# A recurrence in which odd heads change partition halves, so that neighbouring products use different halves of the array's columns

## The chip, the cores and the metric

The kernel runs on one core of one Trainium2 chip. Its engines work side by side: TensorE (PE in the profile; PEld is its loading of weights), VectorE (DVE), ScalarE (ACT), GpSimd (POOL) and SyncE (SP), whose queue issues nearly all DMA loads and stores here. The metric is device time in microseconds (us), as a median over runs.

## The reference

One encoder layer on 1024 tokens of 1024 channels: a half-step SwiGLU block, then two head groups in parallel (four attention heads, and eight heads of an RWKV-7 recurrence with 64 channels each), an output projection, a second SwiGLU block and a norm. What the change touches is the recurrence:

```python
def step(state, inp):
    r_t, w_t, k_t, v_t, aa_t, bb_t = inp
    sa = jnp.einsum('bhvk,bhk->bhv', state, aa_t)
    state = (state * w_t[:, :, None, :] + sa[..., None] * bb_t[:, :, None, :]
             + v_t[..., None] * k_t[:, :, None, :])
    return state, jnp.einsum('bhvk,bhk->bhv', state, r_t)
```

Its state is a 64x64 matrix per head; over the outputs `y` follow a norm per head, a bonus term and a gate. In parallel, attention scores, a softmax and its product with the values are taken in blocks of 128 queries.

## The kernel before

All big weights are streamed from HBM, and most products take several passes over split operands. The stage of the change lies in the middle of the program (lines 1278 to 1482 and the loop over `p` near the end of `tile_layer`).

The 1024 tokens of the recurrence are cut into 16 chunks of 64, worked off in 8 *pairs* `p` of an even (`e` = 0) and an odd (`e` = 1) chunk. Everything about a chunk is precomputed into DRAM, and the class `Pair` loads it: `m1` (decayed receptance and key operands), `TF` (the inverse of the chunk's triangular system), `m3`, and the values `v` twice (into `sv` beside the state, and into `uv` beside the solved rows). `m1` and `TF` have two buffers, by `p % 2`; `m3`, `sv` and `uv` have four for two tiles per pair. So the loads of pair p+2 wait until pair p's last reader, an output product, is done.

`chain` does a step for all 8 heads. Each of its three products contracts 128 partitions and gives 64 rows per head, thus it fills 64 of the array's 128 columns; `rows_of(e)` says which 64 partitions hold the state side `u` and which the value side `v`, and with that which half of the columns a product uses. The three are `ps_z` from `m1` and `sv` (evicted by ACT to `Z`), `ps_z` from `TF` and `Z` (evicted by ACT to `uv`), and `ps_st` from `m3` and `uv` (added by DVE to the next chunk's `sv`, which POOL has filled with the decayed state). Before the change all 8 heads of a step use the same half; the step is cut into two groups of four heads, so that the eviction of one runs beside the products of the other. `outputs` adds two products per head and chunk in `ps_y` (lines 1441 and 1442), in the other half, then norm and gate. `inverse` builds the 64x64 inverses of later pairs from 32x32 blocks with products of 32 columns (`ps_t`).

A scheduler sets the order of instructions on every engine from priorities: `chain` has high priority, and `attend(share)` emits steps of attention (scores `ps_s`, transposes `ps_pt`, values `ps_ov`) so that they fill the time between. The order is fixed when the program is built; each engine and each queue then works in order. When the recurrence and attention are done, `out_in` and `out_proj` (products `ps_wo`) follow.

Of the kernel before, what the change touches and what calls it, by code (L numbers as in the profile page):

```python
# [34 lines left out]
NJ = 4  # L35
# [1242 lines left out]

def rows_of(e):

    return (slice(64, 128), slice(0, 64)) if e == 0 else (slice(0, 64), slice(64, 128))


def half_rows(hh):

    return slice(64 * hh, 64 * hh + 64)
# [40 lines left out]
def inverse(k, pool, p):  # L1329

    nc = k.nc
    x = k.x21[p % 2]
    low = lambda e: slice(64 - 64 * e, 96 - 64 * e)
    high = lambda e: slice(96 - 64 * e, 128 - 64 * e)
    at = lambda e: slice(2 * p + e, 8 * NCH, NCH)
    for e in range(2):
        nc.sync.dma_start(out=x[low(e)], in_=k.xD[at(e), :HL, HL:].rearrange("h s t -> s h t"))
        nc.sync.dma_start(out=k.T11[low(e), :, e], in_=k.tD[at(e)].rearrange("h t c -> t h c"))
        nc.sync.dma_start(out=k.T22[high(e), :, e], in_=k.fD[at(e), HL:, HL:].rearrange("h t c -> t h c"))

    def products(rows, lhs, rhs):
        t = ps(k, "t")[:, : 8 * HL].rearrange("p (h q) -> p h q", q=HL)
        for e in range(2):
            for h in range(8):
                nc.tensor.matmul(t[rows(e), h], lhsT=lhs[:, h], rhs=rhs[:, h, e], start=True, stop=True)  # L1345
        return t

    t = products(high, x, k.T11)
    for e in range(2):
        nc.scalar.copy(out=k.w1[high(e)], in_=t[high(e)])  # L1350
    t = products(low, k.w1, k.T22)
    y = pool.tile([P, 8, HL], F32, name="T12", tag="T12", bufs=1)
    for e in range(2):
        nc.vector.tensor_copy(out=y[low(e)], in_=t[low(e)])
        nc.sync.dma_start(out=k.fD[at(e), :HL, HL:].rearrange("h t c -> t h c"), in_=y[low(e)])


def chain_tools(k, pool):
    k.m1 = [[pool.tile([P, 8, 2, L], F32, name=f"m1{i}{e}") for e in range(2)] for i in range(2)]
    k.TF = [pool.tile([P, 8, P], F32, name=f"TF{i}") for i in range(2)]  # L1360
    k.Z = [pool.tile([P, 8, L], F32, name=f"Z{e}") for e in range(2)]

    k.wl = pool.tile([P, 8, NP2], F32, name="wl")
    for e in range(2):
        for hh in range(2):
            k.nc.gpsimd.tensor_copy(out=k.wl[half_rows(e), hh::2, :], in_=k.WL[half_rows(hh), :, e::2])
        for m in k.m1:
            k.nc.gpsimd.memset(m[e][rows_of(e)[0], :, 0], 0.0)
        k.nc.gpsimd.memset(k.Z[e], 0.0)
    for t in k.TF:  # L1370
        k.nc.gpsimd.memset(t, 0.0)


class Pair:


    def __init__(self, k, pool, p):
        nc = k.nc
        self.k, self.p = k, p
        a, c0 = p // 4, (2 * p) % 8  # L1380
        new = lambda n: [pool.tile([P, 8, L], F32, name=n, tag=n, bufs=4) for _ in range(2)]

        self.m1, self.tf = k.m1[p % 2], k.TF[p % 2]
        for e in range(2):
            u, v = rows_of(e)
            for hh in range(2):
                nc.sync.dma_start(
                    out=self.m1[e][v, hh::2].rearrange("p h s q -> p h (s q)"), in_=k.arD[a][half_rows(hh), :, c0 + e]
                )
            nc.sync.dma_start(out=self.m1[e][u, :, 1], in_=k.akD[a][v, :, p % 4])  # L1390
            nc.sync.dma_start(out=self.tf[u, :, u], in_=k.fD[2 * p + e :: NCH].rearrange("h t c -> t h c"))

        self.m3 = [pool.tile([P, 8, 2, L], F32, name="m3", tag="m3", bufs=4) for _ in range(2)]
        for e in range(2):
            nc.sync.dma_start(out=self.m3[e], in_=k.m3D[a][:, c0 + e])
        self.sv, self.uv = new("sv"), new("uv")
        for e in range(2):
            u, v = rows_of(e)
            for dst in (self.sv[e][u], self.uv[e][v]):
                nc.sync.dma_start(out=dst, in_=k.vD[a][v, p % 4].rearrange("p j (h q) -> p (j h) q", q=L))  # L1400


def chain(k, pool, o, nxt, e):

    nc = k.nc
    hs = [slice(4 * q, 4 * q + 4) for q in range(2)]
    u, v = rows_of(e)
    m1, m3, sv, uv, Z = o.m1[e], o.m3[e], o.sv[e], o.uv[e], k.Z[e]
    after = o.sv[1] if e == 0 else (nxt.sv[0] if nxt else None)

    def products(name, lhs, rhs, then):
        t = h8(ps(k, name))
        for q in hs:
            for h in range(q.start, q.stop):
                nc.tensor.matmul(t[u, h], lhsT=lhs[:, h], rhs=rhs[:, h], start=True, stop=True)  # L1415
            then(q, t[u, q])

    products("z", m1[:, :, 1], sv, lambda q, t: nc.scalar.copy(out=Z[u, q], in_=t))
    if after is not None:
        w = k.wl[v, :, o.p : o.p + 1].broadcast_to([64, 8, L])  # L1420
        nc.gpsimd.tensor_tensor(out=after[u], in0=sv[v], in1=w, op=ALU.mult)
    products("z", o.tf[:, :, u], Z, lambda q, t: nc.scalar.copy(out=uv[u, q], in_=t))
    if after is not None:
        products(
            "st", m3[:, :, 1], uv,
            lambda q, t: nc.vector.tensor_tensor(out=after[u, q], in0=t, in1=after[u, q], op=ALU.add),
        )


def outputs(k, pool, o):  # L1430

    nc = k.nc
    p = o.p
    yp = []

    def output(e):
        if not yp:
            yp.append(h8(ps(k, "y")))
        v = rows_of(e)[1]
        for h in range(8):  # L1440
            nc.tensor.matmul(yp[0][v, h], lhsT=o.m1[e][:, h, 0], rhs=o.sv[e][:, h], start=True, stop=False)  # L1441
            nc.tensor.matmul(yp[0][v, h], lhsT=o.m3[e][:, h, 0], rhs=o.uv[e][:, h], start=False, stop=True)  # L1442

    st = pool.tile([P, 2, 8], F32, name="gst", tag="gst", bufs=3)
    bc = lambda x: x[:, :, None].broadcast_to([P, 8, L])
    yc = pool.tile([P, HB], F32, name="yc", tag="yc", bufs=3)
    a, c = p // 4, slice((p % 4) * P, (p % 4 + 1) * P)

    def last():
        output(1)  # L1450
        nc.vector.tensor_reduce(out=st[:, 0], in_=yp[0], axis=AX.X, op=ALU.add)
        nc.vector.tensor_scalar(out=st[:, 0], in0=st[:, 0], scalar1=1.0 / L, scalar2=None, op0=ALU.mult)
        nc.vector.tensor_tensor(out=h8(yc), in0=yp[0], in1=bc(st[:, 0]), op=ALU.subtract)

    x = []

    def norm():
        x.extend(pool.tile([P, NJ, P], F32, name=n, tag=n, bufs=2) for n in ("lgx", "box"))
        nc.sync.dma_start(out=x[0], in_=k.lgD[a][:, :, c])
        nc.sync.dma_start(out=x[1], in_=k.boD[a][:, :, c])  # L1460
        sq = pool.tile([P, HB], F32, name="ysq", tag="ysq", bufs=1)
        nc.scalar.activation(out=sq, in_=yc, func=AF.Square)
        nc.vector.tensor_reduce(out=st[:, 1], in_=h8(sq), axis=AX.X, op=ALU.add)
        nc.vector.tensor_scalar(
            out=st[:, 1], in0=st[:, 1], scalar1=1.0 / L, scalar2=GN_EPS, op0=ALU.mult, op1=ALU.add
        )
        newton(k, pool, st[:, 1])
        nc.gpsimd.tensor_tensor(out=h8(yc), in0=h8(yc), in1=bc(st[:, 1]), op=ALU.mult)

    def gate():  # L1470
        lg, bo = x
        t = ps(k, "yt")
        for j in range(NJ):
            nc.tensor.transpose(t[:, j * P : (j + 1) * P], yc[:, j * P : (j + 1) * P], k.ident)
        nc.vector.tensor_tensor(out=lg, in0=t.rearrange("p (j q) -> p j q", q=P), in1=lg, op=ALU.mult)
        nc.gpsimd.tensor_tensor(out=lg, in0=lg, in1=bo, op=ALU.add)
        nc.gpsimd.dma_start(out=k.ybD[a][:, :, c], in_=lg)

    return lambda: output(0), last, norm, gate

# [97 lines left out]
def tile_layer(ctx, tc, I, out):  # L1580
# [176 lines left out]
    with pool_("inv", "left") as ip, pool_("chain") as pool:  # L1757
# [3 lines left out]
        inverse(k, ip, 1)  # L1761
        chain_tools(k, pool)
        ops = [Pair(k, pool, 0)]
        nc.gpsimd.memset(ops[0].sv[0][rows_of(0)[1]], 0.0)
        late = None
        for p in range(NP2):
            o = ops.pop(0)
            even, odd, norm, gate = outputs(k, pool, o)
            with tc.high_priority(offset=1500):
                chain(k, pool, o, None, 0)  # L1770
            if p + 2 < NP2:
# [5 lines left out]
            attend((p + 0.45) / 9.2)  # L1777
            with tc.high_priority(offset=1500):
                chain(k, pool, o, ops[0] if ops else None, 1)
            with tc.high_priority(offset=0):  # L1780
                even()
            attend((p + 1.21) / 9.2)

            def late(odd=odd, norm=norm, gate=gate):
                with tc.high_priority(offset=0):
                    odd()
                    norm()
                    gate()

# [127 lines left out]
```

## Time and profile before

| | us |
|---|---|
| median of 3 runs | 2118.7 (2116.01 to 2120.11) |
| profiled execution | 2118.3 |
| its span | 2116.5 |
| PE busy | 2038.9 (96%) |
| DVE busy | 1551.8 (73%) |
| ACT busy | 924.4 (44%) |
| POOL busy | 252.8 (12%) |
| TensorE clock granted, mean | 0.982 |

A row of the profile names the line, the engine, the operation and its tiles as out<-in. A busy PE is not PE at its peak, since products are pipelined: a row with x8 in 0.63 us holds eight products that overlap, and their pace is the distance of the starts. A fp32 product appears as two entries. The whole program's span is told in the page; the stage of the recurrence lies between about 1115 and 1342 us.

### The profile page before, as it was taken

What the parts mean: (1) busy time and instruction counts of PE and PEld (TensorE: products, weight loads), DVE (VectorE), ACT (ScalarE), POOL (GpSimd) and SP (SyncE); (2) the same over time, 40 slices, a digit from 0 to 9 for tenths busy, and PEclk for the clock granted to TensorE, in tenths of its full rate; (3) what the DMA queues carried; (4) which work ended last, traced back from release to release, by engine and by line L of the source; (5) the groups of instructions that cost most, each with busy time, mean ns of one, the idle gap of its engine ahead of it and who ended that gap; (6) DMA issues with size and microseconds to landing.
All of it is one profiled execution on the core that took longest, in us unless ns stands there. A gap on an engine that the chain in (4) does not pass through costs nothing.

```text
span 2116.5 us, 28417 instructions
## 1 busy us (share of the span) xinstructions
PE 2038.9 (96%) x10496; PEld 1650.0 (78%) x10496; DVE 1551.8 (73%) x2718; ACT 924.4 (44%) x1614; POOL 252.8 (12%) x259
## 2 busy tenths in 40 slices
PE   7999999999999999998988999999999999999998
PEld 4788878887888767766767888787888888878887
DVE  6999996579896677889774666576655556599975
ACT  5543343344443466652244444555433333453333
POOL 1100000000001254432133222111000000000001
PEclk8999999999999999999999999999999999999999
DMA  8277732235332124445436764651222222253322
GB/s 330 92 238 242 246 118 94 94 117 183 115 114 95 65 65 122 134 130 139 99 87 157 192 168 137 210 186 37 100 80 82 78 80 90 100 194 110 105 70 80
DMA packets 189771, 273.74 MB, mean 129 GB/s; under 512 B 77504, under 2 KB 121920, under 8 KB 189632
## 3 DMA queue, kind: packets, MB, share of 16 engines
q1 hardware_dynamic: 187920, 268.62, 40.6%
q0 software_dynamic: 1280, 3.15, 0.5%
q8 instruction: 83, 1.36, 0.3%
q14 instruction: 56, 0.46, 0.1%
q10 hardware_dynamic: 432, 0.15, 0.0%
HBM read 202.66 MB, written 66.58 MB: 127 GB/s over the span
## 4 chain that ended last, share of the span: by engine, by line
PE 80%; DVE 11%; DMA 3%; issue 2%; ACT 2%; POOL 1%; SPq 1%; DVEq 0%; ACTq 0%; POOLq 0%
PE ps_w L66 39%; PE ps_dn L66 21%; PE ps_in L66 5%; PE ps_wo L66 4%; DVE Tpr L1317 2%; PE ps_ov L1230 2%; PE ps_z L1415 2%; PE ps_s L66 1%; DVE T L1321 1%; PE ps_pt L1222 1%; PE ps_y L1442 1%; PE ps_y L1441 1%; DVE pair L60 1%; DMA h<-x 1%; PE ps_t L1345 1%
## 5 line engine op out<-in xcount | busy, mean ns | idle before, releaser
L66 PE MATMUL ps_w<-pair 128*128 128x512 f32 x3744 | 877.4, 396 | 13.1 <-ACT pair L59 9.7
L66 PEld LDWEIGHTS ps_w<-pair 128*128 128x128 f32 x3744 | 706.0, 189 | 181.7 <-ACT pair L59 10.3
L66 PE MATMUL ps_in<-pair,win 128*128 128x512 f32 x960 | 253.9, 415 | 8.2 <-DVE acc L1069 4.1
L60 DVE TENSOR_TENSOR pair<-raw,pair 128x512 fp32r<-128x512 f32 x256 | 177.1, 700 | 108.3 <-ACT pair L59 108.2
L59 ACT CAST pair<-raw 128x512 fp32r<-128x512 f32 x256 | 155.4, 621 | 222.3 <-PE ps_w L66 176.8
L66 PE MATMUL ps_dn<-pair 128*128 128x512 f32 x1008 | 236.6, 393 | 2.7 <-DVE part L608 1.7
L66 PEld LDWEIGHTS ps_in<-pair,win 128*128 128x128 f32 x960 | 184.0, 195 | 59.2 <-issue 10.9
L66 PEld LDWEIGHTS ps_dn<-pair 128*128 128x128 f32 x1008 | 188.9, 188 | 47.5 <-DVE part L608 2.5
L66 PE MATMUL ps_dn<-pair,dh 128*128 128x512 f32 (+1 forms) x704 | 204.2, 375 | 0.0
L66 PEld LDWEIGHTS ps_dn<-pair,dh 128*128 128x128 f32 x704 | 128.1, 188 | 25.8 <-issue 0.7
L388 ACT COPY part<-ps_w 128x512 f32<-128x512 f32 x120 | 70.1, 585 | 168.1 <-PE ps_w L66 159.3
L66 PE MATMUL ps_dn<-pair,dl 128*128 128x512 f32 (+1 forms) x352 | 131.2, 375 | 0.0
L551 DVE SCALAR_TENSOR_TENSOR h<-ps_dn,mod,h 128x512 f32<-128x512 f32 (+1 forms) x128 | 90.4, 713 | 37.8 <-PE ps_dn L66 37.5
L59 ACT CAST pair<-hraw 128x512 fp32r<-128x512 f32 x124 | 73.2, 620 | 69.9 <-DMA hraw<-hidD 30.7
L206 POOL TENSOR_TENSOR nacc<-nacc,nsq 128x512 f32<-128x512 f32 x12 | 17.7, 1472 | 666.8 <-ACT nsq L202 666.8
L138 DVE SCALAR_TENSOR_TENSOR wmod<-wmod,cact 128x1024 f32<-128x1024 f32 x68 | 82.8, 1220 | 9.5 <-DMA wmod<-w_mod 9.1
L486 DVE TENSOR_TENSOR t<-ps_w,part 128x512 f32<-128x512 f32 x80 | 54.5, 687 | 46.7 <-PE ps_w L66 28.0
L60 DVE TENSOR_TENSOR pair<-hraw,pair 128x512 fp32r<-128x512 f32 x124 | 82.9, 685 | 5.2 <-ACT pair L59 4.8
L699 POOL TENSOR_TENSOR h<-h,nr 128x256 f32<-128x256 f32 (+1 forms) x6 | 5.4, 915 | 649.0 <-ACT nr L229 649.0
L66 PE MATMUL ps_wo<-pair,woh 128*128 128x512 f32 x256 | 79.8, 393 | 0.0
L66 PEld LDWEIGHTS ps_dn<-pair,dl 128*128 128x128 f32 x352 | 66.3, 188 | 12.8 <-issue 0.2
L481 DVE TENSOR_TENSOR c<-ps_w,part 128x512 f32<-128x512 f32 x80 | 53.3, 685 | 29.5 <-PE ps_w L66 24.4
(348 smaller groups left out, 3089.5 us busy)
## 6 DMA issues: line engine op xcount, KB each, us to landing
wmod<-w_mod SPq DMA_DIRECT2D x68, 512.0 KB, 4.4
raw<-ffn_w_gate SPq DMA_DIRECT2D x44, 512.0 KB, 3.6
raw<-ffn_w_up SPq DMA_DIRECT2D x44, 512.0 KB, 4.5
hidD<-c SPq DMA_DIRECT2D x44, 512.0 KB, 2.7
hraw<-hidD SPq DMA_DIRECT2D x44, 512.0 KB, 3.4
draw<-ffn_w_down SPq DMA_DIRECT2D x40, 512.0 KB, 3.7
h<-x SPq DMA_DIRECT2D x32, 256.0 KB, 4.6
hD<-h SPq DMA_DIRECT2D x32, 256.0 KB, 2.0
```

The lines of the kernel that those rows point to most:

```text
L59: k.nc.scalar.copy(out=hi, in_=src)
L60: k.nc.vector.tensor_tensor(out=lo, in0=src, in1=hi.bitcast(F32), op=ALU.subtract)
L66: k.nc.tensor.matmul(out, lhsT=x, rhs=y, start=start, stop=stop, skip_group_check=onto)
L138: k.nc.vector.scalar_tensor_tensor(out=w, in0=w, scalar=1.0, in1=k.cact, op0=ALU.mult, op1=ALU.mult, accum_out=m)
L388: nc.scalar.copy(out=t, in_=x)
L481: nc.vector.tensor_tensor(out=c[i][:, j], in0=x, in1=y, op=ALU.add)
L486: nc.vector.tensor_tensor(out=t, in0=x, in1=y, op=ALU.add)
L551: nc.vector.scalar_tensor_tensor(out=y, in0=x, scalar=gt[:, d : d + 1], in1=y, op0=ALU.mult, op1=ALU.add)
L1222: nc.tensor.transpose(tp[:, q : q + P], pr[:, s0 + q : s0 + q + P], k.ident)
L1230: nc.tensor.matmul(x.po[:, cols], lhsT=pt[:, b * P : (b + 1) * P], rhs=k.v[b][:, cols], start=b == 0, stop=b == x.i)
L1317: nc.vector.tensor_tensor(out=v, in0=T[:, 0:t, 0:t].rearrange("p s c -> p c s"), in1=xp[:, 0:t, t][:, None, :].broadcast_to([P, t, t]), op ...
L1415: nc.tensor.matmul(t[u, h], lhsT=lhs[:, h], rhs=rhs[:, h], start=True, stop=True)
```

## The change

For odd heads (`hh` = 1) the sides `u` and `v` are exchanged, so that heads h and h+1 of a step give their results to different column halves. A step's product is no longer cut into two groups of heads but issues all eight, alternating; `Z` is one tile of 128 partitions by 4 head pairs, evicted at once; `TF` holds two heads per tile (an even and an odd one, block-diagonal). One of the two evictions to `uv` goes to DVE. The loads of `akD`, `fD`, `m3D` and `vD` are cut by head parity. Output products of both chunks are issued together, alternating by chunk, after the odd chunk. `inverse` loops over heads outside and chunks inside.

```diff
+def rows_of(e, hh=0):
+    return (slice(64, 128), slice(0, 64)) if e == hh else (slice(0, 64), slice(64, 128))
...
     def products(rows, lhs, rhs):
         t = ps(k, "t")[:, : 8 * HL].rearrange("p (h q) -> p h q", q=HL)
-        for e in range(2):
-            for h in range(8):
+        for h in range(8):
+            for e in range(2):
...
             for hh in range(2):
+                u, v = rows_of(e, hh)
...
-            nc.sync.dma_start(out=self.m1[e][u, :, 1], in_=k.akD[a][v, :, p % 4])
-            nc.sync.dma_start(out=self.tf[u, :, u], in_=k.fD[2 * p + e :: NCH].rearrange("h t c -> t h c"))
+                nc.sync.dma_start(out=self.m1[e][u, hh::2, 1], in_=k.akD[a][own, hh::2, p % 4])
+                nc.sync.dma_start(
+                    out=self.tf[e][u, :, u], in_=k.fD[2 * p + e + NCH * hh :: 2 * NCH].rearrange("h t c -> t h c")
+                )
...
-            nc.sync.dma_start(out=self.m3[e], in_=k.m3D[a][:, c0 + e])
+            src = k.m3D[a][:, c0 + e]
+            nc.sync.dma_start(out=self.m3[e][:, 0::2], in_=src[:, 0::2])
+            for dst, own in zip(rows_of(e, 1), rows_of(e)):
+                nc.sync.dma_start(out=self.m3[e][dst, 1::2], in_=src[own, 1::2])
...
-            for dst in (self.sv[e][u], self.uv[e][v]):
-                nc.sync.dma_start(out=dst, in_=k.vD[a][v, p % 4].rearrange("p j (h q) -> p (j h) q", q=L))
+            src = k.vD[a][rows_of(e)[1], p % 4].rearrange("p j (s q) -> p j s q", q=L)
+            for hh in range(2):
+                u, v = rows_of(e, hh)
+                for dst in (self.sv[e][u], self.uv[e][v]):
+                    nc.sync.dma_start(out=dst[:, hh::2], in_=src[:, :, hh])
...
+    sides = [(hh, slice(hh, 8, 2), *rows_of(e, hh)) for hh in range(2)]
+
+    def products(name, lhs, rhs):
+
+        t = ps(k, name)[:, : NJ * L].rearrange("p (j q) -> p j q", q=L)
+        for h in range(8):
+            u = sides[h % 2][2]
+            nc.tensor.matmul(t[u, h // 2], lhsT=lhs(h, u), rhs=rhs(h), start=True, stop=True)
+        return t
+
+    t = products("z", lambda h, u: m1[:, h, 1], lambda h: sv[:, h])
+    z = pool.tile([P, NJ, L], F32, name="Z", tag="Z", bufs=2)
+    nc.scalar.copy(out=z, in_=t)
     if after is not None:
...
+        for hh, hs, u, v in sides:
+            w = k.wl[v, hs, o.p : o.p + 1].broadcast_to([64, NJ, L])
+            nc.gpsimd.tensor_tensor(out=after[u, hs], in0=sv[v, hs], in1=w, op=ALU.mult)
+    t = products("z", lambda h, u: tf[:, h // 2, u], lambda h: z[:, h // 2])
+    for hh, hs, u, v in sides:
+        (nc.vector.tensor_copy if hh else nc.scalar.copy)(out=uv[u, hs], in_=t[u])
     if after is not None:
...
+        t = products("st", lambda h, u: m3[:, h, 1], lambda h: uv[:, h])
+        for hh, hs, u, v in sides:
+            nc.vector.tensor_tensor(out=after[u, hs], in0=t[u], in1=after[u, hs], op=ALU.add)
...
+    def output():
+        yp.append(h8(ps(k, "y")))
         for h in range(8):
...
+            for i, (lhs, rhs) in enumerate(((o.m1, o.sv), (o.m3, o.uv))):
+                for e in range(2):
+                    nc.tensor.matmul(
+                        yp[0][rows_of(e)[1], h], lhsT=lhs[e][:, h, 0], rhs=rhs[e][:, h], start=i == 0, stop=i == 1
+                    )
```

How the order moves, on PE first, at the odd chunk of the first pair. Before: products of a step in fours, output products of one chunk between.

```order
L1442 MATMUL ps_y_9661<-uv_9517,m3_9511 64x64
L1415 MATMUL ps_z_9627<-sv_9516,m101_9483 64x64 x4
L1415 MATMUL ps_z_9639<-Z1_9489,TF0_9486 64x64 x4
L1222 MATMUL ps_pt_8948<-ident_60,pr_8915 128x128 x2
L1441 MATMUL ps_y_9661<-sv_9516,m101_9483 64x64
L1415 MATMUL ps_z_9639<-Z1_9489,TF0_9486 64x64 x4
L1415 MATMUL ps_st_9650<-uv_9518,m3_9512 64x64 x4
L1442 MATMUL ps_y_9661<-uv_9518,m3_9512 64x64
```

The same place now; `sv_9527` and `uv_9529` are of the even chunk, `sv_9528` and `uv_9530` of the odd one.

```order
L1230 MATMUL ps_ov_9040<-v2_8268,pt_9034 128x128
L1424 MATMUL ps_st_9681<-uv_9530,m3_9520 64x64
L1455 MATMUL ps_y_9776<-uv_9530,m3_9520 64x64
L1455 MATMUL ps_y_9776<-sv_9527,m100_9482 64x64
L1455 MATMUL ps_y_9776<-sv_9528,m101_9483 64x64
L1455 MATMUL ps_y_9776<-uv_9529,m3_9519 64x64
L1424 MATMUL ps_st_9681<-uv_9530,m3_9520 64x64 x7
```

The steps come in eights, and the output products of both chunks stand together at the end of the odd chunk.

On SP, the last part of the loads of the second pair (`m3`, `sv`, `uv`; `oD` is a store of attention, `fD<-T12` a result of `inverse`). Before:

```order
L1391 DMA TF1_9487<-fD_129 64x8x64
L1395 DMA m3_9615<-m3D0_114 128x1024
L1395 DMA m3_9616<-m3D0_114 128x1024
L1254 DMA oD0_122<-ot_8944 512x1x128
L1355 DMA fD_129<-T12_9602 32x8x32 x2
L1400 DMA sv_9619<-vD0_118 64x512
L1400 DMA uv_9621<-vD0_118 64x512
L1400 DMA sv_9620<-vD0_118 64x512
L1400 DMA uv_9622<-vD0_118 64x512
```

Now:

```order
L1400 DMA m3_9637<-m3D0_114 128x4x128
L1402 DMA m3_9637<-m3D0_114 64x4x128 x2
L1400 DMA m3_9638<-m3D0_114 128x4x128
L1356 DMA fD_129<-T12_9620 32x8x32 x2
L1402 DMA m3_9638<-m3D0_114 64x4x128 x2
L1254 DMA oD0_122<-ot_9062 512x1x128
L1409 DMA sv_9645<-vD0_118 64x4x64
L1409 DMA uv_9647<-vD0_118 64x4x64
```

The last two rows come twice for each chunk: 26 loads of a pair where there were 14.

At the end of the stage, also on SP: `h` and `wo` are loads of the output projection, `oD` the store of an attention block (`ot`), the seventh of eight blocks before:

```order
L1508 DMA h4_0_11585<-hD0_84 128x512 x2
L1254 DMA oD1_123<-ot_11639 512x1x128
L1508 DMA h6_0_11586<-hD0_84 128x512
L1510 DMA wo_11781<-w_out 128x1024
L1508 DMA h6_0_11586<-hD0_84 128x512
L1510 DMA wo_11817<-w_out 128x1024
```

and the eighth, the last, now:

```order
L1523 DMA h4_0_11701<-hD0_84 128x512 x2
L1254 DMA oD1_123<-ot_11870 512x1x128
L1525 DMA wo_11897<-w_out 128x1024
L1523 DMA h6_0_11702<-hD0_84 128x512 x2
L1525 DMA wo_11933<-w_out 128x1024
```

The first load of `wo` stands behind the store of the last attention block. On PE there are now no score products (`ps_s`) after the last `ps_y`, and 35 rows of them (seven sets of five) before the change.

## Rows read from the trace of the kernel before

**Rows 1.** Windows: stretch, length, then busy us and instructions of each engine, clock, DMA share.

```profile
1132.90:1309.10 176.20, 174.54 (x2147) 152.79 (x2147) 104.76 (x392) 77.99 (x198) 41.47 (x39) 0.99 0.62 160
1309.10:1341.70 32.60, 28.74 (x196) 24.99 (x196) 24.63 (x78) 18.56 (x37) 3.76 (x4) 1.00 0.60 202
1179.98:1189.23 9.25, 9.25 (x115) 7.87 (x116) 6.76 (x28) 4.41 (x11) 2.36 (x4) 1.00 1.00 255
1120.00:1140.00 20.00, 14.80 (x175) 12.99 (x173) 10.06 (x45) 9.38 (x26) 4.61 (x5) 0.82 0.70 171
```

**Rows 2.** Order of time on PE: start us, us, engine, line, what, count.

```profile
1140.76 0.27 PE L1442 MATMUL ps_y<-uv,m 128*64 128x64 f32 x1
1140.81 0.22 PE L1415 MATMUL ps_st<-uv,m 128*64 128x64 f32 x1
1140.87 0.22 PE L1442 MATMUL ps_y<-uv,m 128*64 128x64 f32 x1
1140.87 0.22 PE L1415 MATMUL ps_st<-uv,m 128*64 128x64 f32 x1
...
1146.70 0.63 PE L1415 MATMUL ps_z<-sv,m 128*64 128x64 f32 x8
1147.16 0.63 PE L1415 MATMUL ps_z<-Z,TF 128*64 128x64 f32 x8
1147.72 0.44 PE L1222 MATMUL ps_pt<-ident,pr 128*128 128x128 f32 x2
...
1138.19 1.10 PE L1345 MATMUL ps_t<-T,x 128*32 128x32 f32 x32
```

**Rows 3.** Groups by shape on PE: count, busy us, mean ns, idle before.

```profile
L1442 PE MATMUL ps_y<-uv,m 128*64 128x64 f32 x256 | 33.3, 227 | 0.0
...
L1415 PE MATMUL ps_st<-uv,m 128*64 128x64 f32 x240 | 19.6, 225 | 0.1
...
L1345 PE MATMUL ps_t<-T,w 128*32 128x32 f32 x256 | 10.7, 203 | 0.9 <-ACT w L1350 0.9
```

**Rows 4.** Tile sv: DVE's adds, duration ns min/median/max.

```profile
L1426 DVE TENSOR_TENSOR sv<-ps_st,sv x30: 406/427/429, 1141.3 to 1301.7; 64x256 f32<-64x256 f32 x30
```

**Rows 5.** Lines 1395 and 1400 on SP: issue ns min/median/max; landing of line 1400.

```profile
L1395 SPq DMA_DIRECT2D m<-m3D x16: 375/558/721, 1125.9 to 1268.3; - x16
...
L1400 SPq DMA_DIRECT2D uv<-vD x16: 450/587/913, 1127.6 to 1270.6; - x16
...
DMA to landing us min/median/max: 2.7/5.1/7.0
```

**Rows 6.** SP in order of time, and its waits from 1179 to 1189 us.

```profile
1185.17 0.45 SPq L1337 DMA_DIRECT2D x<-xD  x1
1187.95 0.30 SPq L1339 DMA_DIRECT2D T<-fD  x1
...
SPq L1339 <- DMA m<-m3D: 1.9, 1, 1.9
```

**Rows 7.** PE in order of time, the recurrence's first product.

```profile
1132.89 0.77 PE L1415 MATMUL ps_z<-sv,m 128*64 128x64 f32 x5 [2.80 <-DMA sv<-vD]
```

**Rows 8.** The stage's end: order of time, and lines 1244, 1510, tile woh.

```profile
1328.94 0.44 PE L1222 MATMUL ps_pt<-ident,pr 128*128 128x128 f32 x2 [0.68 <-ACT ot L1252]
...
1340.72 1.06 PE L1230 MATMUL ps_ov<-v,pt 128*128 128x128 f32 x8
...
1327.66 0.60 PE L1250 MATMUL ps_ot<-ident,o 128*128 128x128 f32 x4
...
1328.30 0.58 ACT L1252 COPY ot<-ps_ot 128x512 f32<-128x512 f32 x1 [0.50 <-PE ps_ot L1250]
...
L1244 ACT ACTIVATE o<-o,oss x8: 713/722/724, 1143.0 to 1347.6; 128x512 f32<-128x512 f32 x8
...
DMA to landing us min/median/max: 3.4/4.3/5.8
...
L59 ACT CAST woh<-wo x16: 1034/1050/1054, 1338.7 to 1422.0; 128x1024 fp32r<-128x1024 f32 x16
```

More of the change, by code (lines that the diff above doesn't have):

```diff
@@ L1273, in attention @@
     return [lambda i=i, h=h: step(i, h) for i in blocks for h in range(NH)] + [lambda: step(blocks[-1], NH), lambda: transposed(state[3])]
-def rows_of(e):
-    return (slice(64, 128), slice(0, 64)) if e == 0 else (slice(0, 64), slice(64, 128))
+def rows_of(e, hh=0):
+    return (slice(64, 128), slice(0, 64)) if e == hh else (slice(0, 64), slice(64, 128))
 def half_rows(hh):
@@ L1359, in chain_tools @@
     k.m1 = [[pool.tile([P, 8, 2, L], F32, name=f"m1{i}{e}") for e in range(2)] for i in range(2)]
-    k.TF = [pool.tile([P, 8, P], F32, name=f"TF{i}") for i in range(2)]
-    k.Z = [pool.tile([P, 8, L], F32, name=f"Z{e}") for e in range(2)]
+    k.TF = [[pool.tile([P, NJ, P], F32, name=f"TF{i}{e}") for e in range(2)] for i in range(2)]
     k.wl = pool.tile([P, 8, NP2], F32, name="wl")
@@ L1365, in chain_tools @@
         for hh in range(2):
[L1366 to L1371, printed above, removed]
+            u, v = rows_of(e, hh)
+            k.nc.gpsimd.tensor_copy(out=k.wl[v, hh::2, :], in_=k.WL[half_rows(hh), :, e::2])
+            for m in k.m1:
+                k.nc.gpsimd.memset(m[e][u, hh::2, 0], 0.0)
+    for two in k.TF:
+        for t in two:
+            k.nc.gpsimd.memset(t, 0.0)
 class Pair:
@@ L1384, in __init__ @@
         for e in range(2):
-            u, v = rows_of(e)
+            own = rows_of(e)[1]
             for hh in range(2):
+                u, v = rows_of(e, hh)
                 nc.sync.dma_start(
@@ L1394, in __init__ @@
         for e in range(2):
-            nc.sync.dma_start(out=self.m3[e], in_=k.m3D[a][:, c0 + e])
+            src = k.m3D[a][:, c0 + e]
+            nc.sync.dma_start(out=self.m3[e][:, 0::2], in_=src[:, 0::2])
+            for dst, own in zip(rows_of(e, 1), rows_of(e)):
+                nc.sync.dma_start(out=self.m3[e][dst, 1::2], in_=src[own, 1::2])
         self.sv, self.uv = new("sv"), new("uv")
         for e in range(2):
-            u, v = rows_of(e)
-            for dst in (self.sv[e][u], self.uv[e][v]):
-                nc.sync.dma_start(out=dst, in_=k.vD[a][v, p % 4].rearrange("p j (h q) -> p (j h) q", q=L))
+            src = k.vD[a][rows_of(e)[1], p % 4].rearrange("p j (s q) -> p j s q", q=L)
@@ L1403, in chain @@
+            for hh in range(2):
+                u, v = rows_of(e, hh)
+                for dst in (self.sv[e][u], self.uv[e][v]):
+                    nc.sync.dma_start(out=dst[:, hh::2], in_=src[:, :, hh])
 def chain(k, pool, o, nxt, e):
     nc = k.nc
-    hs = [slice(4 * q, 4 * q + 4) for q in range(2)]
-    u, v = rows_of(e)
-    m1, m3, sv, uv, Z = o.m1[e], o.m3[e], o.sv[e], o.uv[e], k.Z[e]
+    m1, m3, sv, uv, tf = o.m1[e], o.m3[e], o.sv[e], o.uv[e], o.tf[e]
     after = o.sv[1] if e == 0 else (nxt.sv[0] if nxt else None)
[L1411 to L1416, printed above, removed]
@@ L1418, in chain @@
-    products("z", m1[:, :, 1], sv, lambda q, t: nc.scalar.copy(out=Z[u, q], in_=t))
-    if after is not None:
-        w = k.wl[v, :, o.p : o.p + 1].broadcast_to([64, 8, L])
-        nc.gpsimd.tensor_tensor(out=after[u], in0=sv[v], in1=w, op=ALU.mult)
-    products("z", o.tf[:, :, u], Z, lambda q, t: nc.scalar.copy(out=uv[u, q], in_=t))
+    sides = [(hh, slice(hh, 8, 2), *rows_of(e, hh)) for hh in range(2)]
[5 more added lines that the diff above has]
+        return t
@@ L1423, in chain @@
     if after is not None:
[L1424 to L1427, printed above, removed]
+        t = products("st", lambda h, u: m3[:, h, 1], lambda h: uv[:, h])
+        for hh, hs, u, v in sides:
+            nc.vector.tensor_tensor(out=after[u, hs], in0=t[u], in1=after[u, hs], op=ALU.add)
 def outputs(k, pool, o):
@@ L1434, in outputs @@
     yp = []
[L1436 to L1439, printed above, removed]
+    def output():
+        yp.append(h8(ps(k, "y")))
         for h in range(8):
-            nc.tensor.matmul(yp[0][v, h], lhsT=o.m1[e][:, h, 0], rhs=o.sv[e][:, h], start=True, stop=False)
-            nc.tensor.matmul(yp[0][v, h], lhsT=o.m3[e][:, h, 0], rhs=o.uv[e][:, h], start=False, stop=True)
+            for i, (lhs, rhs) in enumerate(((o.m1, o.sv), (o.m3, o.uv))):
[3 more added lines that the diff above has]
+                    )
     st = pool.tile([P, 2, 8], F32, name="gst", tag="gst", bufs=3)
@@ L1449, in last @@
     def last():
-        output(1)
+        output()
         nc.vector.tensor_reduce(out=st[:, 0], in_=yp[0], axis=AX.X, op=ALU.add)
@@ L1477, in gate @@
         nc.gpsimd.dma_start(out=k.ybD[a][:, :, c], in_=lg)
-    return lambda: output(0), last, norm, gate
+    return last, norm, gate
 def out_in(k, pool, y, a):
@@ L1763, in tile_layer @@
         ops = [Pair(k, pool, 0)]
-        nc.gpsimd.memset(ops[0].sv[0][rows_of(0)[1]], 0.0)
+        for hh in range(2):
+            nc.gpsimd.memset(ops[0].sv[0][rows_of(0, hh)[1], hh::2], 0.0)
         late = None
@@ L1767, in tile_layer @@
             o = ops.pop(0)
-            even, odd, norm, gate = outputs(k, pool, o)
+            last, norm, gate = outputs(k, pool, o)
             with tc.high_priority(offset=1500):
@@ L1779, in tile_layer, with late @@
                 chain(k, pool, o, ops[0] if ops else None, 1)
-            with tc.high_priority(offset=0):
-                even()
             attend((p + 1.21) / 9.2)
-            def late(odd=odd, norm=norm, gate=gate):
+            def late(last=last, norm=norm, gate=gate):
                 with tc.high_priority(offset=0):
-                    odd()
+                    last()
                     norm()
```

## The prediction

> **What bounds the kernel now.** The page says that TensorE is busy nearly everywhere, so I went straight to the stage of the change with the windows view, then to the groups by shape, the order of time on PE, the SP queue, and last the end of the stage. From the first product of the recurrence (1132.9 us) to the last output product (1309.1) PE is busy 174.5 of 176.2 us at a clock of 0.99, while DVE has 104.8, ACT 78.0, POOL 41.5 and the DMA engines a share of 0.62 [rows 1]. So PE bounds this stretch, by instruction slots: a fp32 product is two passes, and I call a pass what the trace counts. Eight passes into one half of the columns start 0.46 us before the next eight (1146.70, 1147.16): 57.5 ns each. But where state products (L1415 ps_st, one half) meet output products (L1442, other half), starts come at 1140.76, .81, .87, .87: two passes per 57 ns, 29 ns each [rows 2], though both use all 128 rows. That is what the change wants everywhere.
>
> **Passes.** ps_z and ps_y have two groups each of 256 passes, of which one stands in rows 3, and ps_st has 240 [rows 3]: 1264. At some 30 seams like the one above about three passes are already free, 90 in all (an estimate from that seam and the order). Now (1264 - 90) x 57.5 ns = 67.5 us; alternating, 1264 x 28.75 = 36.3 us. Saved: 31 us. The 512 passes of 32 columns (two groups of 256) run at (1.10 - 0.20)/31 = 29 ns within one column block [rows 2], so alternating may bring between nothing and half, 0 to 8 us. I take 3, below the middle, since 29 ns is also the closest pace that the 64-column rows show. The Trainium skill (TensorE: Matmul & The Clock Gate, "Wait — 56ns, not 53.3ns?") says that starts never come closer than about 25 ns however few columns there are; by it these save at most 512 x 4 ns = 2 us. The trace shows no run of closer starts.
>
> **Switches of shape.** Leaving a 64-column run costs 0.16 us instead of 0.0575 (last pass of 1147.16 at 1147.56, next shape at 1147.72), and entering one costs about the same. In the order of PE the runs of 64-column products that 128-column work follows fall from 63 to 47: 16 x 0.2 to 0.3, I take 4 us. In all PE sheds 38 us.
>
> **Other engines.** Z is evicted once over 128 partitions instead of twice over 64, so ACT does less. One of two uv copies goes to DVE, an operation like the add of 0.43 us [rows 4]: 16 of them, 7 us on an engine with 71 us idle. POOL's decay product is split with the same elements. I cost these at nothing, hidden under PE; where a DVE queue of small operations stands before an add, a step waits up to 1 us, which is inside the 4 us below.
>
> **Loads, what the change adds.** A pair had 14 loads, now 26, of the same bytes: akD, fD and the v rows in halves, m3 in three. An issue of the SP queue takes 0.56 us for 512 KB and 0.59 for 128 KB [rows 5], so size hardly matters: 12 x 0.55 = 6.6 us more per pair (bounds: 12 x 0.30, the shortest issue in rows 6, is 3.6; 12 x 0.6 is 7.2). A pair's SP work is now some 14 x 0.55 plus about ten others at 0.5 = 13 us in a period of 176.2/8 = 22 us; it becomes 19 to 20. The pieces are 256 and 512 bytes long instead of 2 and 4 KB; no row separates sizes, so between nothing and double for 1.5 MB at the 255 GB/s of a saturated load (DMA share 1.00, rows 1), 6 us a pair; I take 2. PE needs (156 - 11)/7 = 20.7 us per pair (next paragraph), so the loads stay just under it; I give 4 us in all for their jitter, bounds 0 and 25. The first pair has no cover: its first product, at 1132.89, had waited 2.8 us for sv [rows 7]. In the new order 16 issues instead of 8 lie between the zeroing of TF and that sv: 8 x 0.55 = 4.4, less one wait that runs beside it: first product at 1136.5.
>
> **The end of the stage.** Before, 32.6 us lie between the last output product and pure ps_wo work [rows 1], and attention fills them. The order of the change has put all score products of this tail ahead of the recurrence's end; what stays is three steps of transposes and values. Before, these ran from 1328.94 to 1341.78, 12.8 us [rows 8]; the other 19.8 us move ahead, some 2 of them before the first product. So the recurrence is 176.2 - 38 + 18 = 156 us of PE, and ends at 1136.5 + 156 + 4 (loads) + 4 (the last two steps have nothing beside them: six hand-overs at 0.6 to 0.7) = 1300.5.
> Then something comes that was hidden. SP's first wo load now stands behind the oD store of the last attention block; before, behind that of the block ahead. That last block must be scaled (last values at 1341.78, o ready at 1348.3: 6.5 us), transposed (0.64), copied (0.58) and stored (an issue of 0.6), then wo lands in 4.3 us and is split in 1.05 [rows 8]: 13.7 us in which PE has four transposes. After such a gap PE runs for a while at the lower of its two levels, 1.2 GHz instead of 2.4: the 20 us of the start, with a gap like it, have a mean of 0.82 [rows 1], which is 3.6 us lost; with one gap of less work I take 2. ps_wo alone starts at 1300.5 + 12.8 + 13.7 + 2 = 1329.0 instead of 1341.7. Everything behind it moves with it: 12.7 us.
>
> **Sum.** The profiled execution took 2118.3 us (span 2116.5), 0.4 below the median of 2118.7. 2118.7 - 12.7 = 2106.
>
> **Rivals.**
> - *The cover holds better.* The values overlap the wait for wo or the o chain ends earlier, and loads cost nothing: 38 less 3.6 for the start, 4 for the steps and 2 to 5 at the end: 2091. For it: DVE and ACT have room. Against it: PE's and SP's orders are fixed, and the store stands before wo.
> - *The loads become the bound (slower).* After 1185.62 SP issued nothing until 1187.95, when an m3 load had landed [rows 6]: the queue holds only some eight loads in flight, and v loads land in 5.1 us, up to 7.0 [rows 5]. With 36 loads a pair, eight in flight: 36 x 5.1/8 = 23 us a pair; at 4.2 us it is 19. The pair after next can't be loaded before this pair's output products, so the wait isn't caught up. Gain and loss meet at a pair of 20.7 + (12.7 + 4)/7 = 23.1 us; at 24.5 the time is 2118.7 + 7 x 1.4 = 2128. For it: a DMA share of 1.00 in a load burst. Against it: halves land sooner than wholes, and most bursts had slack.
> - *The alternation does little.* The mechanism: loading of weights for the other half waits for the running pass, and 29 ns holds only over a seam of a few passes. Then 34 of the 38 us are missing: 2140. Against it: the pairs of starts in rows 2; no row shows more than six in a sequence. The Trainium skill (the same page, "The mechanism") says that loading overlaps a running product only when the row groups differ, and here they don't; it speaks for this rival, and the trace of the seam against it.
>
> **Chances.** Forecast 0.50, better cover 0.22, loads 0.21, little 0.07. The forecast's own range is 2097 to 2116; with the others 2089 to 2125 holds eight in ten. About 0.2% (4 us) can be told from no change. Faster by more: nearly all of the first two and a fifth of the loads' case, 0.74. Within: 0.02 of the forecast and 0.07 of the loads, 0.09. Slower: the rest of the loads' case and the last, 0.17.
>
> **What would show it.** ps_z, ps_st and ps_y starting in pairs, 29 ns per pass, over whole groups of 16; fewer than 95% busy PE between first and last recurrence product; SP busy for most of that stretch; no score products after the last ps_y, and a gap of some 12 us on PE before the first ps_wo with a lower clock behind it. It is wrong if that gap is short (then faster), if PE waits on "DMA sv<-vD" at several pairs (then slower), or if passes of a group stay 57 ns apart.

## The result: slower by 0.7%

| | before | after |
|---|---|---|
| median of 4 runs | 2119.4 us (2116.01 to 2120.53) | 2134.1 us (2131.0 to 2137.12) |
| ratio | | 1.0071, 95% interval 1.0055 to 1.0088 |
| span of the profiled execution | 2116.5 | 2129.1 |
| PE busy, clock granted | 2038.9, 0.982 | 2017.1, 0.976 |

TensorE works less and the program takes longer. The windows of the changed kernel, first product to last output product and from there to the first ps_wo, answer to [rows 1]; the third line holds both stretches, and the fence behind it has the same for the kernel before.

```profile
1135.00:1327.30 192.30, 166.84 (x2240) 140.53 (x2241) 120.15 (x441) 72.26 (x178) 42.80 (x53) 0.93 0.58 147
1327.30:1352.00 24.70, 10.81 (x88) 9.36 (x84) 15.39 (x47) 11.48 (x21) 4.04 (x5) 0.82 0.69 222
1135.00:1352.00 217.00, 177.65 (x2321) 149.89 (x2321) 135.54 (x488) 83.73 (x199) 46.84 (x57) 0.92 0.60 155
```

```profile
1132.90:1340.20 207.30, 201.78 (x2331) 176.36 (x2331) 128.21 (x470) 96.04 (x235) 45.24 (x43) 0.99 0.62 168
```

PE's busy time fell by 24.1 us (201.8 to 177.7), but its idle time grew from 5.5 to 39.4, so the stretch is 9.7 us longer, and it began 2.1 us later. The profiled execution of the change is the fastest of its four (2131.0 us), so its trace shows a little less than the difference of the medians.

The alternation itself works. PE in order of time (start, us) against [rows 2]: 14 passes of ps_z in 0.65 us, where 8 took 0.63. The last row, 27 us on, is the first product of the next pair.

```profile
1187.78 0.24 PE L1424 MATMUL ps_z<-sv,m 128*64 128x64 f32 x1 [1.62 <-DMA sv<-vD]
1187.79 0.27 PE L1455 MATMUL ps_y<-sv,m 128*64 128x64 f32 x1
1187.86 0.22 PE L1424 MATMUL ps_z<-sv,m 128*64 128x64 f32 x1
1187.89 0.22 PE L1455 MATMUL ps_y<-sv,m 128*64 128x64 f32 x1
1188.19 0.65 PE L1424 MATMUL ps_z<-sv,m 128*64 128x64 f32 x14
1188.77 0.81 PE L66 MATMUL ps_s<-kn,qh 128*128 128x512 f32 x2
1189.38 0.63 PE L66 MATMUL ps_s<-kn,ql 128*128 128x512 f32 x1
1189.81 0.63 PE L1197 MATMUL ps_s<-kr,qr 128*128 128x512 f32 x1
...
1214.93 0.33 PE L1424 MATMUL ps_z<-sv,m 128*64 128x64 f32 x2 [0.75 <-DMA sv<-vD]
```

The same groups by shape (count, busy us, mean ns, idle before) as in [rows 3]: a ps_y group has 21.5 us busy instead of 33.3, ps_st 14.6 instead of 19.6.

```profile
L1455 PE MATMUL ps_y<-uv,m 128*64 128x64 f32 x256 | 21.5, 227 | 0.0
L1424 PE MATMUL ps_z<-sv,m 128*64 128x64 f32 x256 | 16.0, 241 | 10.5 <-DMA sv<-vD 7.3 <-DVE nwt L245 1.6 <-DVE sv L1440 0.9
L1424 PE MATMUL ps_st<-uv,m 128*64 128x64 f32 x240 | 14.6, 235 | 4.5 <-DVE uv L1436 2.6 <-ACT uv L1436 1.9
```

What sets the pace is seen where the pairs begin: at 1187.78 and 1214.93, 27 us apart, the first product waits for sv, which only just landed. With the pairs counted from 0, the distance over pairs 1 to 7 is 25.0 us (1163.1 to 1313.2); before the change it was 22.4 (1155.1 to 1289.3). PE's waits for sv in the stretch (us in total, times, longest):

```profile
PE ps_z L1424 <- DMA sv<-vD: 7.3, 5, 3.1
```

SP in order of time, answering to [rows 5, 6], shows why sv is late.

```profile
1168.84 0.53 SPq L1389 DMA_DIRECT2D m<-arD  x1
1169.41 0.61 SPq L1392 DMA_DIRECT2D m<-akD  x1
1170.07 0.61 SPq L1393 DMA_DIRECT2D TF<-fD  x1
...
1194.60 0.58 SPq L1389 DMA_DIRECT2D m<-arD  x1
...
1201.19 0.61 SPq L1392 DMA_DIRECT2D m<-akD  x1
1204.82 0.57 SPq L1254 DMA_DIRECT2D oD<-ot  x1
...
1211.42 0.57 SPq L1409 DMA_DIRECT2D sv<-vD  x1
1212.04 1.63 SPq L1409 DMA_DIRECT2D uv<-vD  x1
1213.71 0.62 SPq L1409 DMA_DIRECT2D sv<-vD  x1
1214.37 0.61 SPq L1409 DMA_DIRECT2D uv<-vD  x1
...
L1409 SPq DMA_DIRECT2D sv<-vD x32: 573/607/1398, 1131.8 to 1312.4; - x32
...
L1402 SPq DMA_DIRECT2D m<-m3D x32: 573/607/1427, 1127.5 to 1307.7; - x32
```

SP hardly rests: an issue of a load starts some 0.65 us after the one before, 0.61 of issue and mostly 0.04 to the next. Between the first load of pair 2 (1168.84) and that of pair 3 (1194.60) it issues 37 transfers, 23.4 us of issue in 25.8 us, without a pause of more than 0.2 us. In the next pair, a store that waits for its data holds the queue on top (oD, 3.0 us at 1201.8). Before, there were on average 24 issues a pair, 13.8 us in 21.3. Two other reasons for a late load, a buffer that isn't free and a queue that is full, are not seen in this trace. Between the first and the last product, SP never waits longer than 1.0 us for a product of PE, which is how a buffer comes free (up to 3.6 before). And counted at the end of each issue from 1130 to 1310 us, at most seven of SP's transfers are on their way, four in the median; before the change eight was the most, and at 1185.62, where the prediction saw SP stand still, it was eight.

The end of the stage answers to [rows 8]: PE waits for the scaled o, then for wo.

```profile
1338.17 1.06 PE L1230 MATMUL ps_ov<-v,pt 128*128 128x128 f32 x8
1344.33 1.12 PE L1250 MATMUL ps_ot<-ident,o 128*128 128x128 f32 x4 [5.10 <-ACT o L1244]
1352.01 0.79 PE L66 MATMUL ps_wo<-pair,woh 128*128 128x512 f32 x1 [6.57 <-ACT woh L59]
```

### The profile page after: what moved, and what is told of

The parts are those of the page before. It is cut to its first block, busy times and chain, and to the rows that moved or that the text cites. A ratio compares the mean times of both kernels' runs of the same rounds, so it can differ in the third digit from the quotient of the medians.

```text
span 2129.1 us, 28518 instructions
## 1 busy us (share of the span) xinstructions
PE 2017.1 (95%) x10496; PEld 1624.4 (76%) x10496; DVE 1560.7 (73%) x2734; ACT 913.1 (43%) x1582; POOL 255.9 (12%) x279
## 4 chain that ended last, share of the span: by engine, by line
PE 72%; DVE 15%; DMA 6%; issue 3%; ACT 2%; SPq 2%; POOL 0%; DVEq 0%; ACTq 0%; POOLq 0%
PE ps_w L66 32%; PE ps_dn L66 20%; PE ps_in L66 5%; PE ps_wo L66 4%; DVE Tpr L1318 2%; DVE wmod L138 2%; DVE pair L60 2%; DMA wmod<-w_mod 2%; PE ps_s L66 1%; PE ps_ov L1230 1%; DVE T L1322 1%; PE ps_x L951 1%; PE ps_z L1424 1%; PE ps_pt L1222 1%; DMA sv<-vD 1%
## 5 line engine op out<-in xcount | busy, mean ns | idle before, releaser
L59 ACT CAST pair<-hraw 128x512 fp32r<-128x512 f32 x124 | 73.4, 620 | 69.8 <-DMA hraw<-hidD 30.3
```

The source lines that it names most:

```text
L59: k.nc.scalar.copy(out=hi, in_=src)
```

## Experiments

Three theories were put up. A: the number of issues on SP is the bound. B: the transfers are, the same bytes in small pieces. C: turn-around, the longer chain of hand-overs and the buffers. Each time is a median; the ratio is to runs of the kernel before on the same chip.

**The loads alone, in the kernel before.**

```diff
...
-            nc.sync.dma_start(out=self.m3[e], in_=k.m3D[a][:, c0 + e])
+            src = k.m3D[a][:, c0 + e]
+            nc.sync.dma_start(out=self.m3[e][:, 0::2], in_=src[:, 0::2])
+            for r in rows_of(e):
+                nc.sync.dma_start(out=self.m3[e][r, 1::2], in_=src[r, 1::2])
...
```

> The kernel before with only the loads of the change: akD, fD and v in halves by head parity, m3 in three pieces, 26 loads per pair instead of 14, into the same places as before (no exchange of halves, products as before). Theory A and B alike (the loads alone are what costs): SP needs 25 to 26 us per pair against PE's 22.3, so the stage ends 7 x 3 = 21 us later: 2140 (2133 to 2146), with PE waiting for sv at most pairs. Theory C (the longer chain, the merged output products or the exchange costs, not the loads): 2119 +- 3.

2136.3 us, 1.0083 (1.0070 to 1.0096): the loads alone cost as much as the whole change, with the products, the chain and the buffers of the kernel before. So C falls. Pairs come 26.5 us apart (1157.6 to 1316.8). The first products wait for sv here too, but not for long, since more of attention's products stand between them (2258 products from the first to the last of the recurrence, 2147 before). PE's waits (us, times, longest):

```profile
PE ps_z L1423 <- DMA sv<-vD: 4.6, 5, 1.9
```

**The same pieces, eight of them issued by another engine.**

```diff
-                    nc.sync.dma_start(out=dst[:, hh::2], in_=src[:, :, hh])
+                    nc.gpsimd.dma_start(out=dst[:, hh::2], in_=src[:, :, hh])
```

> The changed kernel with the eight loads of v per pair issued by POOL instead of SP; bytes, pieces and buffers are the same. Theory A (SP's issue pace is the bound: 36 issues of 0.65 us and 3 us of waits make the 25 to 26 us between first products of neighbouring pairs): 28 issues x 0.65 + 3 = 21.2 us, so pairs come 21 to 22 us apart, PE is what they wait for, and the time falls by 7 x 4 = 28 us to 2107 (2100 to 2115). Theory B (the transfers are the bound: the same bytes in pieces of 256 and 512 bytes keep the DMA engines busy): the pieces are the same, so pairs stay 25 us apart, 2134 +- 3. Theory C (turn-around: loads of a pair wait for the output products two pairs before, and the chain of hand-overs is longer): nothing changes either, 2134 +- 3.

2109.3 us, 0.9952 (0.9938 to 0.9966): 25 us less than the change as it was, and faster than before. Pairs 1 to 7 begin 20.8 us apart (1156.4 to 1281.2). Bytes, pieces and buffers are those of the change, so B falls and A stands. Its window, and its longest PE waits:

```profile
1131.70:1330.50 198.80, 176.49 (x2332) 145.72 (x2331) 140.34 (x501) 84.49 (x204) 79.51 (x109) 0.96 0.71 172
```

```profile
PE ps_ot L1250 <- ACT o L1244: 7.6, 2, 7.4
PE ps_t L1346 <- DVE lgx L1490: 4.2, 1, 4.2
PE ps_t L1346 <- DMA x<-xD: 3.7, 2, 3.6
```

No wait for sv is among them. PE is busy 176.5 us, as in the change, and idle 22.3.

**ACT instead of POOL** (`nc.scalar` in the same line).

> The same eight loads issued by ACT. Theory A: pairs 21 to 22 us apart as with POOL, but ACT has 8 x 0.6 = 5 us of issues per pair between the evictions of Z and uv that the chain waits for, at worst one issue in front of each of four: 0 to 2.4 us per pair back, 2107 to 2122. Theories B and C: 2134 +- 3, or more by the ACT delays.

2132.3 us, 1.0065 (1.0052 to 1.0077), above the 2107 to 2122 that theory A gave. By the trace, ACT's own work now stands behind its issues. The longest wait, 8.8 us before an eviction of Z, begins with 3.2 us in which the queue waits for a product to free a buffer (from 1206.0); five issues follow, and at its end Z waits for its own products. ACT's waits:

```profile
ACT Z L1429 <- DMA uv<-vD: 17.3, 3, 8.8
...
ACT uv L1436 <- DMA uv<-vD: 6.2, 2, 3.8
```

PE itself waited longest for loads of m3 (6.9 us, 4 times), so that ACT's waits are what took the gain back is read from the trace and not shown.

**No alternation, twice: with v on POOL and with all on SP.**

```diff
-        for h in range(8):
+        for h in (0, 2, 4, 6, 1, 3, 5, 7):
             u = sides[h % 2][2]
...
-        for h in range(8):
-            for i, (lhs, rhs) in enumerate(((o.m1, o.sv), (o.m3, o.uv))):
-                for e in range(2):
+        for e in range(2):
+            for h in (0, 2, 4, 6, 1, 3, 5, 7):
+                for i, (lhs, rhs) in enumerate(((o.m1, o.sv), (o.m3, o.uv))):
```

> As with the v loads on POOL, but without the alternation: a step's eight products go to the even heads first and then to the odd ones, and the output products of one chunk before those of the other. Places, loads, evictions and instruction counts stay; ps_t still alternates. Theory 1 (with the loads out of the way PE bounds the stage, and the alternation is what that kernel gains): the passes of z, y and st are 57 ns apart again, their starts sum to 14 + 8 + 2 = 24 us more, time 2131 (2122 to 2138). Theory 2 (the stage is bound by hand-overs or still by loads, the passes only fill waits): 2109 +- 4.

> The changed kernel, all loads on SP as it has them, but without the alternation (even heads first, then odd; one chunk's output products before the other's). With v on POOL the same edit cost 15 us. If the loads on SP alone set the pace of the changed kernel, PE's 23 us of slower passes fit into waits that are there anyway: 2134 to 2140 (pairs stay 25 us apart). If PE still sets the pace in good part: 2149 (2144 to 2155).

With v on POOL: 2124.2 us, 1.0018 (1.0008 to 1.0028), 15 us above 0.9952. With all on SP: 2137.4 us, 1.0082 (1.0069 to 1.0094), which the intervals can't tell from the change's 1.0071. So the alternation is worth 15 us where PE sets the pace, and next to nothing where SP does: in the trace of the latter PE is busy 195.5 us from the first product to the first ps_wo, instead of 177.7 with the alternation, and the stretch is as long (217.9 us against 217.0). Groups without it, with v on POOL, and with it:

```profile
L1455 PE MATMUL ps_y<-uv,m 128*64 128x64 f32 x256 | 33.4, 229 | 0.0
...
L1424 PE MATMUL ps_z<-Z,TF 128*64 128x64 f32 x256 | 15.3, 227 | 0.3 <-ACT Z L1429 0.3
```

```profile
L1455 PE MATMUL ps_y<-uv,m 128*64 128x64 f32 x256 | 25.0, 229 | 0.0
...
L1424 PE MATMUL ps_z<-Z,TF 128*64 128x64 f32 x256 | 11.0, 226 | 0.0
```

**The parts that need no new loads, in the kernel before:** v on POOL (its one v line), the loop of `inverse` exchanged as in the change, and both.

> The kernel before, its four v loads per pair issued by POOL. Theory 1 (SP had room before, 13 us of issues in 22): loads landed ahead anyway, 2119 +- 4. Theory 2 (moving loads off SP is a gain by itself, whatever the products do): 2109 to 2114, and then the alternation has little part in the 2109 of the changed kernel with v on POOL.

> The kernel before with the loop over heads and chunks in inverse exchanged, so that its products of 32 columns alternate between two blocks of columns, and nothing else changed. By the changed kernel's trace a pass of ps_t goes from 32 to 25 ns; 512 passes: 3.5 us less on PE, which bounds this stage: 2116 (2114 to 2118). Rival: the passes of the seam fill in (another order of PE, or waits in their place): 2119 +- 2.

> The kernel before with v on POOL and the loop of inverse exchanged, both of which gained alone (6 and 4 us): if they add up, 2109 (2107 to 2112), which is what the whole change with v on POOL reaches; then the exchange of halves has so far paid only for its own loads. Rival: the two gains are one (both let the first pair start earlier): 2113.

2113.1 us, 0.9968 (0.9957 to 0.9978); 2115.3 us, 0.9976 (0.9964 to 0.9988); both 2110.3 us, 0.9956 (0.9943 to 0.9969). Within the intervals they add up. POOL's 6 us was not expected by theory A: 2.4 of them are the first product, at 1130.5 instead of 1132.9; the rest is not settled. The two reach what the whole change with v on POOL reaches, so what else the change brings nets to nothing: the alternation's 15 us are spent on its twelve more loads, the steps that are no longer cut in two, or the new order at the end. No run separates these.

**The wo load freed of the oD store** (the last block's store on POOL).

```diff
-        nc.sync.dma_start(out=k.oD[a][:, :, c], ...)
+        (nc.gpsimd if x.i == 7 else nc.sync).dma_start(out=k.oD[a][:, :, c], ...)
```

> The changed kernel with the store of the last attention block issued by POOL, so that the first wo load no longer stands behind it on SP. If the end of the stage is as the trace of the changed kernel reads (first wo load 11 us late behind that store): the second gap on PE (6.6 us before the first ps_wo) goes, the first (5.1 us, for the scaled o) stays, and 6 to 7 us come back: 2127 (2125 to 2129). Rival: the wo products then wait for the split of wo or for their other operand: 2131 to 2134.

2134.6 us, 1.0067 (1.0053 to 1.0080): nothing. SP's longest wait at the end now names what the store had covered: wo's buffers are those of the yraw tiles, whose split on DVE (L1512) stands behind the last block's scaling.

```profile
SPq L1525 <- DVE pair L1512: 10.9, 2, 10.0
```

**More on POOL:** the loads of norm and gate as well, or m3 as well.

> v loads and the two loads of norm and gate (lgD, boD) on POOL. In the kernel with only v on POOL, PE waited 4.2 us for a DVE queue held by a late lgD load, and 3.6 us for a late load of the inverse; SP sheds two more issues per pair. If SP's backlog in the first pairs is what is left: 2104 (2100 to 2107). Rival: on POOL the loads of norm and gate stand in front of the decay products that the chain waits for, and take back what they give: 2109 to 2114.

> The changed kernel with v and m3 loads on POOL: 14 of 26 per pair, SP keeps 22 issues per pair (14.4 us). If SP's backlog in the first two pairs is what costs the kernel with v alone on POOL its 3.6 and 4.2 us of PE waits: 2103 (2099 to 2107). Rival: 14 x 0.64 = 9 us of issues per pair on POOL stand in front of the decay products of the chain, as with ACT's evictions: 2109 to 2120.

2115.6 us, 0.998 (0.9969 to 0.999), and 2129.1 us, 1.0044 (1.0031 to 1.0057): both slower than with v alone on POOL, and above the ranges of their rivals too. In the first, by the trace, the idle POOL queue issued lgD and boD of two pairs ahead of need; in that stretch the DMA engines have no room (share 1.15 as counted), the loads of the inverse landed late (6.3 to 7.5 us after their issue, against 2.2 to 4.9 with v alone on POOL), and PE waited 7.6 us in the first pair. That this is what cost the 6 us was not tested. Its window and wait (the row names boD; for PE's weight load of the same product it is x of the inverse):

```profile
1134.00:1144.00 10.00, 1.73 (x22) 1.22 (x22) 2.46 (x12) 1.50 (x5) 5.06 (x7) 0.66 1.15 225
```

```profile
PE ps_t L1346 <- DMA box<-boD: 7.6, 1, 7.6
```

In the second, the recurrence began at 1146.1 and the first ps_wo waited 17.7 us for woh; no mechanism was tested.

**Halves exchanged in DRAM**, so that a pair has 18 loads: all on SP, then v on POOL, then with the extra stores on ACT (all 88, not 56 as the expectation says).

```diff
...
-            for dst, own in zip(rows_of(e, 1), rows_of(e)):
-                nc.sync.dma_start(out=self.m3[e][dst, 1::2], in_=src[own, 1::2])
+            nc.sync.dma_start(out=self.m3[e], in_=k.m3D[a][:, c0 + e])
...
+            nc.sync.dma_start(out=to[:, :, 0], in_=m[:, :, 0])
+            for i in range(2):
+                nc.sync.dma_start(out=to[half_rows(1 - i), :, 1], in_=m[half_rows(i), :, 1])
...
```

> The changed kernel with the exchange of halves made where the operands are written to DRAM: m3D holds odd heads with halves exchanged, vD holds each chunk's values in both halves. A pair then has 18 loads instead of 26 (m3 two, v four), all on SP; the products are those of the change. The stage before it has 64 + 24 more stores. Theory A (number of issues on SP): 28 issues x 0.65 + 3 = 21.2 us per pair, the same as with v on POOL: 2109 (2103 to 2114). Theory B (transfers: bytes): the values are now loaded twice over, 3.6 instead of 3.1 MB with the rest, so pairs stay at 25 us: 2134 +- 4. Rival: the stores delay the stage before: 2115 or more with a later first product.

> The same with the four v loads on POOL: 14 loads per pair on SP and 4 on POOL, 24 issues x 0.65 = 16 us on SP. If the issue queue is what the change lost its gain to, nothing of it is left; the first pairs lose the waits for late loads of the inverse too (3.6 and 4.2 us with v alone on POOL): 2104 (2099 to 2108). If the order of the work (steps not cut into two groups, output products merged, the end of the stage) costs the rest: 2109 to 2113.

> As the kernel with halves exchanged in DRAM and v on POOL (14 loads per pair on SP), but its 56 of 88 extra stores that SP issued in the stage before now stand on ACT, behind the ACT copies that make their data. In that kernel the recurrence itself, first product to first ps_wo, took 195.8 us against 198.8 with v on POOL alone, but it began 17 us later, since PE had waited 22.6 us near 1020 us in the stage before. If SP's extra stores there are the cause: the first product comes at about 1132 again, time 2106 (2102 to 2111). Rival: the bytes of the extra stores, or ACT's issues, hold that stage as much: 2118 to 2128.

2134.4 us, 1.0074 (1.0061 to 1.0087); 2125.5 us, 1.0028 (1.0017 to 1.0039); 2123.1 us, 1.0018 (1.0006 to 1.0029). Inside the stage theory A held: with more bytes but 18 loads a pair, all of them on SP, pairs come 21.0 us apart (1176.0 to 1301.8), and first to last product takes 172.8 us against 192.3. But the stage begins at 1155.2 instead of 1135.0: PE waited in the stage before, where the extra stores are. Window and longest PE wait of the first of the three:

```profile
1000.00:1050.00 50.00, 21.82 (x91) 16.68 (x90) 28.94 (x58) 8.14 (x14) 3.00 (x3) 0.69 0.50 109
```

```profile
PE ps_in L66 <- ACT sq L1073: 22.6, 1, 22.6
```

With v on POOL and the stores still on SP that wait was 20.4 us and the stage began at 1149.2; with the stores on ACT it was 8.5 us, and the stage began at 1139.3, but took 6 us longer (201.7 against 195.8 to the first ps_wo). By the traces SP's issues were part of the cause; the times of the two can't be told apart, and the rest stays open.

The fastest kernels are the change with v on POOL (0.9952) and the kernel before with v on POOL and the inverse alternating (0.9956).

## Why the prediction was wrong, point by point

- **Loads: the step that failed.** SP's work for a pair "becomes 19 to 20" us, PE needs 20.7, "so the loads stay just under it", and 4 us were given in all (bounds 0 and 25). The pair took 25.0 us, and moving eight issues off SP gave back 25 us, the outer bound. Of the 5 us a pair that were missing, 1.7 are the issues themselves: 35.3 of them took 21.7 us on average, where 36 were to take 20, since the loads mostly took 0.61 us and not 0.55. The other 3.3 lie between the issues and had no term at all: some 0.06 us on the mean from one to the next, 2.2 us a pair, and waits inside the queue like oD's 3 us, 1.1 a pair. A sum that ends 1 us under the bound should have had those. PE's side of the comparison was right: with v on POOL pairs come 20.8 us apart.
- **The rival "loads become the bound"** named the result and its price: meeting at 23.1 us a pair, 25.0 gives 2118.7 + 7 x 1.9 = 2132 for a measured 2134. Its sign came true as well, waits of PE for sv at several pairs. Its mechanism was wrong. It took a queue that is full at eight loads in flight, and their landing; but landing got shorter (a median of 2.8 us over SP's issues against 4.0 before), no more than seven were in flight, and with eight issues moved to POOL pairs came faster although landing took 3.8. The issue is the price.
- **Passes and switches.** By the distances of starts, before against the change with v on POOL: 1095 passes of 64 columns at close distance (under 80 ns) took 58.1 us, now 1074 take 30.3, 28 ns each: 28 us saved where 31 were forecast. The switches failed: 166 distances of 80 to 300 ns, 21.2 us, became 182, 23.2 us, where 4 us less were forecast. With ps_t that makes 29 of the 38 us; PE's busy time fell by 24 to 25, at a lower clock (0.92 and 0.96 against 0.99). Not all of it is time won: without the alternation, v on POOL, the close distances take 56.5 us instead of 30.3, and the kernel only 15 us more, since PE is idle less (16.9 us against 22.3) and has more clock (0.98 against 0.96).
- **ps_t.** 3 us forecast; 4 measured alone, and 11.0 us of close distances became 7.4.
- **First pair.** Forecast 1136.5, measured 1135.0. That is close, in part by luck: the kernel with the last store on POOL, whose edit lies at the stage's end, began at 1139.8.
- **The end.** From the last output product to ps_wo 28.5 us forecast, 24.7 measured, with the gap on PE and the low clock (0.82 in that stretch). The cause was only half seen: the store stands before the wo load, but wo's buffers come free no earlier, and with the store gone nothing was won.
- **The rival "alternation does little"** fell with the groups of 14 in 0.65 us.

With the loads out of the way (v on POOL), the forecast of 2106 was missed by 3 us. That is partly luck: the first product came 4.8 us earlier than forecast, first to last product took 172.9 us instead of 164, and the end 25.9 instead of 28.5; and POOL gave 6 us to the kernel before as well, which the forecast did not have.

## What to carry to other kernels

Before an operand is cut into more loads, add up the issuing queue per period: count every issue on it, at the distance of two starts and not at the issue's own length, and add the waits of what else stands in it. If that comes near the bound, the queue can be the bound. Moving loads to another queue is no gain by itself: here eight a pair on POOL won 25 us and the same eight on ACT next to nothing, and two more on POOL lost 6 again. Moving work to an earlier stage needs room there too.

## What the runs showed that was not expected

- An issue on SP took 0.61 us for 64 KB as for 128 KB (lines 1409 and 1402 above), and the next mostly began 0.04 us later: about 1.5 loads per us. On POOL a v load took about the same (mean 638 ns).

```profile
L1409 POOL DMA_DIRECT2D uv<-vD x26 | 16.2, 638 | 0.7 <-PE ps_s L1198 0.7
```

- Passes in alternating halves don't start evenly: most distances are 5 or 50 ns, 28 ns on the mean, and in ps_t 5, 25 or 45 ns, 20 on the mean (v on POOL), though all 128 rows are used.
- Behind the PE gap of 1.6 us before 1187.78 the granted clock fell: over 1188 to 1192 us it is 0.66, that is for most of it 1.2 GHz instead of 2.4, and the score products of 512 columns start 0.43 us apart (1189.38, 1189.81 above). At a clock of 1.00 it is 0.23 us (1212.73 and 1212.96). So part of what such a gap costs stands behind it, as busy time.
